# The whole decoder trunk put into one block that the scheduler orders on its detailed timing model

## The chip, the cores and the metric

The kernel runs on one core of a Trainium2 chip. The metric is the device time of one execution in microseconds (us). Three timed runs of the kernel before took 2652.8, 2655.67 and 2657.19 us; the median is 2655.67 us. Everything below that is called "the trace" comes from one further, profiled execution, whose first and last instruction are 2656.2 us apart.

## The reference, cut to what matters

The program is a decoder trunk of two layers over 1024 tokens of width 1024, all in float32. Each layer is a mixing sub-layer and a feed-forward sub-layer, and both take scale, shift and gate vectors from a condition vector `c`.

```
cond = silu(c)
for l in range(DEPTH):
    mod = cond @ w_mod[l] + b_mod[l]
    sh1, sc1, gt1, sh2, sc2, gt2 = split(mod, 6)
    h = rms_norm(x, norm_g[l, 0]) * (1.0 + sc1) + sh1
    y = mixer_block(h, ...)
    x = x + gt1 * rms_norm(y, norm_g[l, 1])
    h = rms_norm(x, norm_g[l, 2]) * (1.0 + sc2) + sh2
    y = square(relu(h @ w_up[l])) @ w_down[l]
    x = x + gt2 * rms_norm(y, norm_g[l, 3])
```

`mixer_block` projects `h` once and feeds four groups: a short gated convolution, an attention with a compressed, a selected and a window branch ("nsa"), a gated linear attention ("gla") and a gated MLP over 128 positions ("gmlp"). The four outputs are normalised, joined and sent through `w_o`.

## The kernel before, in words

**Tiling.** Tokens are cut into two halves of 512 (`hf` 0 and 1), and activations are held transposed, 128 features by 512 tokens. A matrix product is `gemm`: for each half of the weight rows `wunit` loads a 128x512 block (256 KB) by a DMA on SP's queue (L152), ScalarE rounds it to a high part (L161, CAST) and VectorE takes the low part by a subtraction (`sub`, L125). `mm3` (L167 to L169) then issues three matmuls of 512 columns for each block of 128 rows: high by high, high by low, low by high. So each weight unit of 12 matmuls needs one load, one ScalarE and one VectorE instruction before it. For a layer's mixer, `raw_a` or `raw_b` has 3 buffers and the split tiles 4; for the feed-forward `raw_f` has 4 and `w_f` 6.

**Stages.** The last lines of `trunk_kernel` (L961 to L975) give the program order: the mixer of layer 0 for half 0, then for half 1, a run of modulation columns, then feed-forward and mixer in turn: ff(0,0), mix(1,0), ff(0,1), mix(1,1), ff(1,0), ff(1,1). `mix` ends with the product by `w_o`, a root-mean-square norm (the matmul by `ones`, L189), `residual` (L134, L131) and the norm that makes the feed-forward's input. `ff` has 32 hidden groups: `up` makes one, `down` adds four of them to the eight output tiles `y`; it ends with the same norm and `residual`.

**Modulation columns.** `mod_col` computes 128 entries of `mod` on VectorE: two loads of 256 KB from `w_mod`, each followed by a multiply-and-reduce (L232, shown in the trace as CUSTOM_DVE_ANT_0 and in the order as ISA, with a second short instruction that reads the accumulator), and one small instruction (L134) that adds both and the bias. The first 32 reduces (`mw`, 12 buffers) come before anything else. The other 160 (`mr`, 2 buffers) are `mods(0, (2, 3, 4))` inside the first mixer, and `mods(0, (5,))` and `mods(1, range(6))` after the second: their results are needed only at the first residual and later.

**What sets the order.** The code is written stage by stage, and the Tile scheduler orders it. It walks a model of the machine through time and, on each engine, sends the ready instruction that stands earliest in program order (`high_priority` shifts this for some). The result is a fixed order for each engine's queue: on the chip an instruction waits until all before it on its engine have gone. SP's queue issues all loads and stores in one such order; a load that needs a free buffer holds up all the loads behind it.

Attention's last step is `attend`: four transposes of the weights through TensorE (L699), the cast of the result on ScalarE (L701), the low part on VectorE (L125), and two matmuls with the values (L704 for the high part, L705 for the low part).

Of the kernel before, what the change touches and what calls it, by code (L numbers as in the profile page):

```python
# [35 lines left out]
def trunk_kernel(ctx, tc, xT, c, pos, freq, sel, w_in, conv_w, cmp_pos, cmp_w1, cmp_w2,  # L36
                 gla_w2, gla_b, gmlp_ws, gmlp_b, gains, w_o, norm_g, w_mod, b_mod,
                 w_up, w_down, out):
    nc = tc.nc
    V, A, P, PE = nc.vector, nc.scalar, nc.gpsimd, nc.tensor  # L40
    dma = nc.sync.dma_start

# [12 lines left out]
    def ps(tag, shape=(128, 512)):  # L55
        return psum.tile(list(shape), F32, name="ps_" + tag, tag=tag,
                         bufs={"mm": 2, "ff": 2, "s": 2, "t": 1, "pv": 1}[tag])
# [9 lines left out]

    A.preload_act_table_set("natural_log_exp_and_others")

# [1 line left out]
    ident = const.tile([128, 128], F32, name="ident")  # L71
    ones = const.tile([128, 128], F32, name="ones")
    bones = const.tile([128, 128], F32, name="bones")
# [19 lines left out]
    P.affine_select(out=cm[:, 384:512], in_=cm[:, 384:512], pattern=[[-1, 128]],  # L93
                    compare_op=ALU.is_ge, fill=NEG, base=0, channel_multiplier=1)

# [1 line left out]
    par = []  # L97
    for l in range(DEPTH):
        d = {}
# [8 lines left out]
        for n in names:  # L108
            dma(out=par[l][n], in_=src[n][l])

# [1 line left out]
    KS = const.tile([128, 1024], F32R, name="KS")  # L112
    KW = const.tile([128, 1024], F32R, name="KW")
    VS = const.tile([128, 8, 128], F32R, name="VS")
# [5 lines left out]
    st_carry = const.tile([128, 64], F32, name="st_carry")  # L120
    V.memset(KC, 0.0)

# [1 line left out]
    def sub(out, a, b):  # L124
        V.tensor_tensor(out=out, in0=a, in1=b, op=ALU.subtract)  # L125

# [97 lines left out]
            add(yk, yk, xo(k)[:, cs])  # L224
            dma(out=xnew[:, k, cs], in_=yk)

# [1 line left out]
    def mod_col(l, j, k, mk):  # L228
        mp = work.tile([128, 2], F32, name="mp", tag="mp", bufs=4)
        for kh in range(2):  # L230
            raw = mk(w_mod[l, 8 * j + k, :, kh * T:kh * T + T], [128, T])
            V.tensor_tensor_reduce(out=raw, in0=raw, in1=cond[kh], scale=1.0, scalar=0.0,  # L232
                                   op0=ALU.mult, op1=ALU.add, accum_out=mp[:, kh:kh + 1])
        stt(par[l]["mod"][:, j, k:k + 1], mp[:, 0:1], mp[:, 1:2], par[l]["bmod"][:, 8 * j + k:8 * j + k + 1],
            ALU.add, ALU.add)
# [43 lines left out]
                mod_col(l, j, k, mk)  # L279
            mod_scale(l, j, slice(0, 8))  # L280

# [1 line left out]
    cosd = dram.tile([2, 128, T], F32, name="cosd")  # L283
    sind = dram.tile([2, 128, T], F32, name="sind")

# [43 lines left out]
                    A.copy(o, p)  # L329
                    dma(out=dst[hf], in_=o)  # L330

# [1 line left out]
    CONV0, GMLP0, GLA0, NSA0 = 0, 6, 10, 17  # L333

    def conv_part(l, hf, h, rg, lane, st_):
# [232 lines left out]
    def nsa_part(l, hf, h, rg, gates):  # L568
# [24 lines left out]
        A.copy(kvt[:, 16:528], p)  # L593
        if hf == 0:
            V.tensor_copy(cmp_halo, kvt[:, 512:528])
        # rotary embedding
        cos, sin = (rg.tile([128, T], F32, name="cs", tag="q", bufs=4) for _ in range(2))
        dma(out=cos, in_=cosd[hf])
        dma(out=sin, in_=sind[hf])
# [77 lines left out]
        for j in range(4):  # L677
# [53 lines left out]
            def gate(bi):  # L731
                return gates[:, j, :].rearrange("p (h b) -> p h b", b=3)[:, :, bi:bi + 1]

            # selected (every causal block) and window branches
            def branch(bi, KX, VX, pieces, far, h0, nh, last):
                two = far or len(pieces) == 2
                NM, L = small((128, nh, 2)), small((128, nh, 2))
# [53 lines left out]
            else:  # L791
                branch(1, KS, VS, [(0, 4), (4, i - 3)], False, 0, 4, False)
            branch(2, KW, VW, [(max(0, i - 3), min(i + 1, 4))], i >= 4, 0, 4, False)
            # compressed branch
            sp = ps("s", (128, 4, 64))
            for k in range(2):
                PE.matmul(sp[:, 2 * k:2 * k + 2, 0:ns], qs[:, k, tj], KC[:, :, 0:ns],
# [19 lines left out]
                add(yr, pr[64:128], yr)  # L817
        return [yN[:, 0, :], yN[:, 1, :]]

# [1 line left out]
    xa = [dram.tile([2, 128, 8, T], F32, name=f"xa{l}") for l in range(DEPTH)]  # L821
    xb = dram.tile([2, 128, 8, T], F32, name="xb")
    h2 = {}
# [10 lines left out]
    def mix(l, hf, h, between=None):  # L834
        d = par[l]
        gain = d["gain"]
        with ExitStack() as es:
            gr = es.enter_context(region("gates"))
            if l == 0 and hf == 0:
                sx = ("ff", "ff", "ff")  # L840
                with region("wb", "right") as lane_pool["b"]:
                    with region("gl", "right") as rg:
                        gates, lrT = gate_part(l, hf, h, gr, rg, "a")
                        rope_tables()
                        yn = nsa_part(l, hf, h, es.enter_context(region("ns")), gates)
                        ol = gla_part(l, hf, h, rg, "b", sx, lrT)
                    with region("cv", "right") as rg, region("gm", "right") as rg2:
                        og = gmlp_part(l, hf, h, rg2, "b", sx)
                        oc = conv_part(l, hf, h, rg, "b", sx)
                    mods(0, (2, 3, 4))  # L850
                lane_pool["f"] = pool("ff", side="right")
            else:
                sx = ("s", "t", "pv")
                with region("cv") as rg, region("gm") as rg2:
                    oc = conv_part(l, hf, h, rg, "a", sx)
                    og = gmlp_part(l, hf, h, rg2, "a", sx)
                with region("gl") as rg:
                    gates, lrT = gate_part(l, hf, h, gr, rg, "a")
                    ol = gla_part(l, hf, h, rg, "a", sx, lrT)
                yn = nsa_part(l, hf, h, es.enter_context(region("ns")), gates)  # L860
            on = group_out(yn, "t", gain[:, 2:4])
            outs = [split(t) for t in oc + og + ol + on]
# [200 lines left out]
```

## Time and profile before

| | |
|---|---|
| median of three timed runs | 2655.67 us |
| profiled execution, first to last instruction | 2656.2 us |
| TensorE matmul busy | 2513.5 us (95%), 11690 records |
| TensorE weight load busy | 1989.3 us (75%) |
| VectorE busy | 1680.0 us (63%) |
| ScalarE busy | 1310.3 us (49%) |
| GpSimd busy | 56.5 us (2%) |
| mean granted TensorE clock | 0.985 |
| DMA, mean over the span | 114 GB/s |

The page gives no other time of the profiled execution than its span, which is 0.5 us above the median. PE is TensorE's matmul, PEld its weight load, which runs beside it; DVE is VectorE, ACT ScalarE, POOL GpSimd, SP the engine that issues the DMAs. A busy time counts a stretch in which at least one instruction of the engine is in flight. The columns of each view are told at its first group below.

### The profile page before, as it was taken

Reading aid. Unit: us, or ns where it says so; the run is one execution under the profiler, and the core shown is the slowest. Engines: PE = TensorE matmul, PEld = TensorE weight load, DVE = VectorE, ACT = ScalarE, POOL = GpSimd, SP = SyncE. Lnnn points to the kernel's source line nnn. Section 1 sums busy time; section 2 is a strip of 40 time slices with the busy share of each in tenths; the row PEclk is TensorE's granted clock in tenths of the full one; section 3 lists DMA queues with packets and bytes.
Section 4 is the critical chain, followed back from the end, with each engine's and each line's share of the span. In section 5 each row is a group of like instructions: output and inputs, shape, how many; then the busy total and the mean of one; then the engine's idle time right before and its main releaser. Section 6 shows DMA issues by size and latency. Waiting matters only on the chain.

```text
span 2656.2 us, 34273 instructions
## 1 busy us (share of the span) xinstructions
PE 2513.5 (95%) x11690; PEld 1989.3 (75%) x11690; DVE 1680.0 (63%) x3540; ACT 1310.3 (49%) x2649; POOL 56.5 (2%) x65
## 2 busy tenths in 40 slices
PE   2899879999999999999999999999999999999998
PEld 1676657677778887767788887777777888788887
DVE  7797987888574448457674446547876544534446
ACT  3474534468654345356653435345775443434343
POOL 0100000200000000010000000001000000000000
PEclk9999989999999999999999999999999999999999
DMA  7435566511343334222243334222123333533332
GB/s 270 138 97 174 192 204 202 179 53 36 100 142 98 96 99 143 82 71 69 95 144 100 96 97 145 88 61 89 40 76 121 98 96 99 179 97 98 96 99 84
DMA packets 168937, 301.56 MB, mean 114 GB/s; under 512 B 20453, under 2 KB 24122, under 8 KB 168762
## 3 DMA queue, kind: packets, MB, share of 16 engines
q1 hardware_dynamic: 168762, 299.37, 36.3%
q8 instruction: 92, 1.51, 0.2%
q14 instruction: 83, 0.68, 0.1%
HBM read 281.47 MB, written 17.83 MB: 113 GB/s over the span
## 4 chain that ended last, share of the span: by engine, by line
PE 76%; DVE 10%; ACT 4%; DMA 4%; issue 2%; POOL 0%; DVEq 0%; SPq 0%; ACTq 0%; POOLq 0%
PE ps_ff L168 16%; PE ps_ff L169 16%; PE ps_ff L167 16%; PE ps_mm L167 6%; PE ps_mm L169 6%; PE ps_mm L168 6%; DMA mr<-in_w_mod_dram 3%; PE ps_pv L705 1%; PE ps_pv L704 1%; DVE mr L232 1%; PE ps_mm L699 1%; ACT bp L754 1%; PE ps_t L189 1%; PE ps_s L744 1%; DVE w_a L125 1%
## 5 line engine op out<-in xcount | busy, mean ns | idle before, releaser
L161 ACT CAST w_f<-raw_f 128x512 fp32r<-128x512 f32 x504 | 313.3, 622 | 649.7 <-PE ps_ff L168 638.6
L125 DVE TENSOR_TENSOR w_f<-raw_f,w_f 128x512 fp32r<-128x512 f32 x504 | 348.7, 692 | 261.6 <-ACT w_f L161 254.7
L169 PE MATMUL ps_ff<-h,w_f 128*128 128x512 f32 x1024 | 405.9, 397 | 17.1 <-DVE w_f L125 17.1
L167 PE MATMUL ps_ff<-h,w_f 128*128 128x512 f32 x1024 | 404.8, 396 | 4.8 <-ACT h L203 4.8
L168 PE MATMUL ps_ff<-h,w_f 128*128 128x512 f32 x1024 | 406.6, 397 | 0.6 <-DVE h L134 0.4
L167 PE MATMUL ps_ff<-hid,w_f 128*128 128x512 f32 x992 | 388.9, 392 | 0.1
L168 PE MATMUL ps_ff<-hid,w_f 128*128 128x512 f32 x992 | 388.6, 392 | 0.0
L169 PE MATMUL ps_ff<-hid,w_f 128*128 128x512 f32 x992 | 388.2, 391 | 0.0
L167 PE MATMUL ps_mm<-h,w_a 128*128 128x512 f32 x832 | 336.4, 405 | 34.8 <-ACT w_a L161 30.5
L169 PE MATMUL ps_mm<-h,w_a 128*128 128x512 f32 x832 | 332.7, 400 | 11.7 <-DVE w_a L125 11.6
L168 PE MATMUL ps_mm<-h,w_a 128*128 128x512 f32 x832 | 338.8, 409 | 0.9 <-DVE h L125 0.9
L131 DVE TENSOR_TENSOR y<-y,ps_ff 128x512 f32<-128x512 f32 (+1 forms) x232 | 154.9, 668 | 238.0 <-PE ps_ff L169 237.1
L161 ACT CAST w_a<-raw_a 128x512 fp32r<-128x512 f32 x208 | 128.6, 618 | 233.0 <-PE ps_mm L168 216.2
L169 PEld LDWEIGHTS ps_ff<-h,w_f 128*128 128x128 f32 x1024 | 195.0, 190 | 60.1 <-DVE w_f L125 18.8
L125 DVE TENSOR_TENSOR w_a<-raw_a,w_a 128x512 fp32r<-128x512 f32 x208 | 143.3, 689 | 152.2 <-ACT w_a L161 146.0
L167 PEld LDWEIGHTS ps_ff<-h,w_f 128*128 128x128 f32 x1024 | 195.4, 191 | 47.6 <-ACT h L203 6.5
L168 PEld LDWEIGHTS ps_ff<-h,w_f 128*128 128x128 f32 x1024 | 195.0, 190 | 45.2 <-issue 2.7
L167 PEld LDWEIGHTS ps_mm<-h,w_a 128*128 128x128 f32 x832 | 158.0, 190 | 81.2 <-ACT w_a L161 33.6
L167 PEld LDWEIGHTS ps_ff<-hid,w_f 128*128 128x128 f32 x992 | 186.6, 188 | 40.5 <-issue 1.4
L168 PEld LDWEIGHTS ps_ff<-hid,w_f 128*128 128x128 f32 x992 | 186.7, 188 | 39.1 <-issue 1.0
L169 PEld LDWEIGHTS ps_ff<-hid,w_f 128*128 128x128 f32 x992 | 186.7, 188 | 37.8 <-issue 0.5
L169 PEld LDWEIGHTS ps_mm<-h,w_a 128*128 128x128 f32 x832 | 157.9, 190 | 55.8 <-DVE w_a L125 15.1
(350 smaller groups left out, 3586.4 us busy)
## 6 DMA issues: line engine op xcount, KB each, us to landing
raw_f<-in_w_up_dram SPq DMA_DIRECT2D x256, 256.0 KB, 2.7
raw_f<-in_w_down_dram SPq DMA_DIRECT2D x256, 256.0 KB, 2.6
mr<-in_w_mod_dram SPq DMA_DIRECT2D x160, 256.0 KB, 3.0
raw_a<-in_w_in_dram SPq DMA_DIRECT2D x144, 256.0 KB, 2.8
raw_a<-in_w_o_dram SPq DMA_DIRECT2D x64, 256.0 KB, 2.9
mw<-in_w_mod_dram SPq DMA_DIRECT2D x32, 256.0 KB, 4.4
bp<-in_cmp_w_dram SPq DMA_DIRECT2D x32, 256.0 KB, 4.6
raw_b<-in_w_in_dram SPq DMA_DIRECT2D x32, 256.0 KB, 3.0
```

Source lines behind the costliest of these rows:

```text
L125: V.tensor_tensor(out=out, in0=a, in1=b, op=ALU.subtract)
L131: eng.tensor_tensor(out=out, in0=a, in1=b, op=ALU.add)
L161: A.copy(hi, raw)
L167: PE.matmul(ps_ap, wh, xh, start=start, stop=False)
L168: PE.matmul(ps_ap, wh, xl, start=False, stop=False)
L169: PE.matmul(ps_ap, wl, xh, start=False, stop=stop)
L189: PE.matmul(p, ones, acc, start=True, stop=True)
L232: V.tensor_tensor_reduce(out=raw, in0=raw, in1=cond[kh], scale=1.0, scalar=0.0, op0=ALU.mult, op1=ALU.add, accum_out=mp[:, kh:kh + 1])
L699: PE.transpose(tp[0:kn, hh, :], cols(h0 + hh), ident)
L704: PE.matmul(pv[:, h0:h0 + nh, :], vst, th[0:kn], start=first[0], stop=False)
L705: PE.matmul(pv[:, h0:h0 + nh, :], vst, tl[0:kn], start=False, stop=last)
L744: PE.matmul(sp[:, 0:w], qh[:, h0 + hh, :], KX[:, 128 * k0:128 * k0 + w], start=True, stop=False)
```

## The change

One line is added at the start of `trunk_kernel`. It opens a block that is closed when the function ends, and asks the scheduler to order what is traced in it on the timeline model instead of the plain one. No instruction is added or taken away, no tile changes its size or its number of buffers. The other eight hunks of the diff empty a comment line each, so the line numbers of the changed kernel are higher by one.

```diff
@@ -37,6 +37,7 @@
                  gla_w2, gla_b, gmlp_ws, gmlp_b, gains, w_o, norm_g, w_mod, b_mod,
                  w_up, w_down, out):
     nc = tc.nc
+    ctx.enter_context(tc.block(schedule_with_timeline_sim=True))
     V, A, P, PE = nc.vector, nc.scalar, nc.gpsimd, nc.tensor
     dma = nc.sync.dma_start
 
@@ -67,7 +68,7 @@
 
     A.preload_act_table_set("natural_log_exp_and_others")
 
-    # ---- constants ----
+
     ident = const.tile([128, 128], F32, name="ident")
...
```

All 11,105 matmuls of the program are the same and every engine's queue holds the same work in another order. Three places show how.

**VectorE, after the gates of the first mixer.** These rows follow VectorE's subtraction for `gates` (the last line of `logsig`). In the kernel before, weight splits (`w_a`, `w_b`) and attention's keys stand there; `mr` is a modulation reduce, `cond` its other factor, `mp` its sum.

```order
L134 SCALAR_TENSOR_TENSOR gates<-ps_t,gtmp 128x48
L125 TENSOR_TENSOR w_a<-raw_a,w_a 128x512 x2
L125 TENSOR_TENSOR w_b<-raw_b,w_b 128x512 x2
L590 MEMSET kvt 128x16
L595 COPY cmp_halo<-kvt 128x16
L125 TENSOR_TENSOR w_a<-raw_a,w_a 128x512 x2
L603 STREAM_SHUFFLE p<-p 128x512
L131 TENSOR_TENSOR p<-p 128x512
L613 CAST KS<-p 64x512
L615 CAST KW<-p 64x512
L125 TENSOR_TENSOR KS<-p,KS 64x512
L125 TENSOR_TENSOR KW<-p,KW 64x512
```

In the changed kernel the same place reads:

```order
L135 SCALAR_TENSOR_TENSOR gates<-ps_t,gtmp 128x48
L318 TENSOR_SCALAR sc<-n 128x8x8
L233 ISA mr,mp<-mr,cond_126 128x512
L233 ISA mp 128x1
L126 TENSOR_TENSOR w_a<-raw_a,w_a 128x512
L233 ISA mr,mp<-mr,cond_127 128x512
L233 ISA mp 128x1
L135 SCALAR_TENSOR_TENSOR mod_101<-mp,bmod_97 128x1
L126 TENSOR_TENSOR w_a<-raw_a,w_a 128x512
L233 ISA mr,mp<-mr,cond_126 128x512
L233 ISA mp 128x1
L126 TENSOR_TENSOR g<-g 128x512
```

Modulation reduces have moved up between the weight splits, and behind these rows nine more follow with only three small instructions between them. In both orders the first matmul of the first feed-forward stands as number 1164 on TensorE; ahead of it VectorE has 86 of the 160 `mr` reduces before and all 160 now. The rest of VectorE's work ahead of that matmul is the same, but for the small instructions that belong to those reduces.

**VectorE, at the end of the first feed-forward.** `y` with `G` is the scaling of `residual`, `y` with `xo` its addition, and each `w_f` is a weight split for the next feed-forward's matmuls, which TensorE has at this point. Before:

```order
L125 TENSOR_TENSOR w_f<-raw_f,w_f 128x512
L134 SCALAR_TENSOR_TENSOR y<-y,G_104,nt 128x512 x2
L131 TENSOR_TENSOR y<-y,xo 128x512 x2
L134 SCALAR_TENSOR_TENSOR y<-y,G_104,nt 128x512 x2
L131 TENSOR_TENSOR y<-y,xo 128x512 x2
L134 SCALAR_TENSOR_TENSOR y<-y,G_104,nt 128x512 x2
L131 TENSOR_TENSOR y<-y,xo 128x512 x2
L134 SCALAR_TENSOR_TENSOR y<-y,G_104,nt 128x512 x2
L131 TENSOR_TENSOR y<-y,xo 128x512 x2
L131 TENSOR_TENSOR nt<-nt 128x512
L125 TENSOR_TENSOR hid<-r,hid 128x512
```

And in the changed kernel:

```order
L126 TENSOR_TENSOR w_f<-raw_f,w_f 128x512 x2
L135 SCALAR_TENSOR_TENSOR y<-y,G_105,nt 128x512 x8
L126 TENSOR_TENSOR w_f<-raw_f,w_f 128x512
L132 TENSOR_TENSOR y<-y,xo 128x512 x4
L126 TENSOR_TENSOR w_f<-raw_f,w_f 128x512
L132 TENSOR_TENSOR y<-y,xo 128x512 x4
L126 TENSOR_TENSOR w_f<-raw_f,w_f 128x512
```

Before, sixteen residual instructions stood in one piece; now weight splits stand after the eighth, the twelfth and the sixteenth. The end of the second feed-forward reads the same in each order; at the end of the third the sixteen stand in one piece in both.

**TensorE, in the second mixer's attention.** `ps_t` and `ps_mm` with `ident` are transposes of attention weights, `ps_pv` the products with the values, `ps_s` the scores, and `ps_ff` the feed-forward of the other half. Before, in the second mixer:

```order
L704 MATMUL ps_pv<-w_a,VS 128x512
L699 MATMUL ps_mm<-ident,bp 128x128 x4
L765 MATMUL ps_s<-KW,qh 128x128
L766 MATMUL ps_s<-KW,ql 128x128
L705 MATMUL ps_pv<-w_a,VS 128x512
L704 MATMUL ps_pv<-w_a,VS 128x512
L699 MATMUL ps_t<-ident,bp 128x128 x4
```

In the changed kernel, in the third:

```order
L700 MATMUL ps_mm<-ident,bp 128x128 x2
L745 MATMUL ps_s<-KS,qh 128x384
L700 MATMUL ps_mm<-ident,bp 128x128 x6
L747 MATMUL ps_s<-KS,ql 128x384
L170 MATMUL ps_ff<-hid,w_f 128x512
L168 MATMUL ps_ff<-hid,w_f 128x512
L169 MATMUL ps_ff<-hid,w_f 128x512
L170 MATMUL ps_ff<-hid,w_f 128x512
L168 MATMUL ps_ff<-hid,w_f 128x512
L169 MATMUL ps_ff<-hid,w_f 128x512
```

Feed-forward matmuls now stand between the steps of attention, eight more of them behind the last row shown. In program order the feed-forward comes after the second mixer; before, a tenth of the first feed-forward's matmuls stood ahead of number 2133, now ahead of number 1619. The last 1635 matmuls, those of the last feed-forward, stand alone at the end in both.

## Rows read from the trace of the kernel before

**Rows 1.** The page, its head and part 1 (busy us, share of the span, instructions).

```profile
span 2656.2 us, 34273 instructions
...
PE 2513.5 (95%) x11690; PEld 1989.3 (75%) x11690; DVE 1680.0 (63%) x3540; ACT 1310.3 (49%) x2649; POOL 56.5 (2%) x65
```

**Rows 2.** Stretches (columns: length, each engine's busy us and instructions, TensorE clock, DMA).

```profile
0.00:361.30 361.30, 277.88 (x1313) 204.78 (x1313) 299.65 (x818) 182.33 (x397) 14.98 (x23) 0.96 0.56 179
361.30:560.00 198.70, 183.70 (x909) 136.98 (x909) 164.54 (x419) 86.43 (x180) 14.59 (x14) 0.97 0.55 172
560.00:2600.00 2040.00, 2007.69 (x9194) 1607.99 (x9192) 1180.03 (x2225) 1020.32 (x2031) 26.92 (x28) 0.99 0.32 97
...
850.00:900.00 50.00, 50.00 (x223) 41.40 (x222) 20.62 (x31) 20.05 (x34) 0.00 (x0) 1.00 0.33 97
```

**Rows 3.** Timeline of TensorE at the first feed-forward's first matmul (start us, duration, instruction).

```profile
361.28 1.22 PE L167 MATMUL ps_ff<-h,w_f 128*128 128x512 f32 x2 [3.52 <-ACT h L203]
```

**Rows 4.** Busy time of the mr tiles' instructions on VectorE, by stretch.

```profile
0.00:361.30 361.30, 59.29 (x86) 0.96 0.56 179
361.30:560.00 198.70, 51.31 (x74) 0.97 0.55 172
```

**Rows 5.** One tile, mr (durations min/median/max in ns, times; waits; landing).

```profile
L232 DVE CUSTOM_DVE_ANT_0 mr<-mr,cond x160: 647/686/1200, 82.2 to 544.5; 128x512 f32<-128x512 f32 x160
...
  DMA mr<-in_w_mod_dram: 36.6, 49
...
DMA to landing us min/median/max: 2.4/3.0/5.7
```

**Rows 6.** VectorE's waits to 361.3 us (total us, times, longest us).

```profile
DVE mr L232 <- DMA mr<-in_w_mod_dram: 18.7, 25, 2.0
DVE w_a L125 <- ACT w_a L161: 13.6, 4, 7.1
```

**Rows 7.** Waits of SP's DMA queue from 73 to 361.3 us.

```profile
SPq L275 <- DVE mp L232: 89.7, 61, 13.9
```

**Rows 8.** Timeline of VectorE around two reduces.

```profile
233.07 0.69 DVE L232 CUSTOM_DVE_ANT_0 mr<-mr,cond 128x512 f32<-128x512 f32 x1
...
233.68 0.68 DVE L392 TENSOR_REDUCE var<-sq 128x8 f32<-128x512 f32 x1
...
235.58 0.22 DVE L134 SCALAR_TENSOR_TENSOR mod<-mp,bmod 128x1 f32<-128x1 f32 x1
235.71 0.69 DVE L232 CUSTOM_DVE_ANT_0 mr<-mr,cond 128x512 f32<-128x512 f32 x1
```

**Rows 9.** Timeline of VectorE at the end of the first feed-forward.

```profile
1020.00 1.41 DVE L134 SCALAR_TENSOR_TENSOR y<-y,G,nt 128x512 f32<-128x512 f32 x2
...
1031.93 0.68 DVE L125 TENSOR_TENSOR w_f<-raw_f,w_f 128x512 fp32r<-128x512 f32 x1
```

**Rows 10.** Waits of TensorE over the span.

```profile
PE ps_ff L169 <- DVE w_f L125: 17.1, 4, 5.5
```

**Rows 11.** Timeline of TensorE at the same place as rows 9.

```profile
1026.79 0.39 PE L168 MATMUL ps_ff<-h,w_f 128*128 128x512 f32 x1
1032.66 0.80 PE L169 MATMUL ps_ff<-h,w_f 128*128 128x512 f32 x1 [5.49 <-DVE w_f L125]
1033.26 0.63 PE L167 MATMUL ps_ff<-h,w_f 128*128 128x512 f32 x1
1033.68 0.63 PE L168 MATMUL ps_ff<-h,w_f 128*128 128x512 f32 x1
```

**Rows 12.** Two stretches: that transition, and the third mixer's attention.

```profile
1010.00:1050.00 40.00, 34.52 (x136) 26.21 (x135) 33.37 (x53) 22.96 (x40) 0.00 (x0) 0.91 0.52 171
1050.00:1350.00 300.00, 294.19 (x1444) 228.33 (x1445) 184.14 (x422) 163.39 (x368) 12.55 (x13) 0.98 0.26 81
```

**Rows 13.** Timeline of TensorE in the second mixer's attention.

```profile
604.78 1.03 PE L699 MATMUL ps_mm<-ident,bp 128*128 128x128 f32 x8
...
606.12 0.48 PE L704 MATMUL ps_pv<-w_a,VW 128*128 128x512 f32 x1
```

## The prediction

> **What bounds the kernel now.** I began with the page's busy times. TensorE's matmul is busy for 2513.5 of 2656.2 us, its weight load for 1989.3 [rows 1]. The first figure suggests that no more than 143 us can be gained. To see whether a busy TensorE is also a fast one, I took a stretch inside the first feed-forward with nothing but its products: 223 matmuls in 50.00 us, one each 224 ns, with the weight load busy 41.40 us, 82.8% [rows 2]. I use that share as a yardstick: the weight-load time of a stretch, divided by 0.828, is an estimate of what its matmuls take undisturbed, and what the stretch takes beyond that I call excess.
>
> The Trainium skill ("Trainium Kernel Development and Optimization", section "Performance Expectations") calls matmul busy time a bad measure, since matmuls are pipelined, and weight-load time a good one. By the first, 32 us are to be had after 560 us, by the second 98; the trace agrees so far as the steady stretch shows 100% by the one and 82.8% by the other.
>
> The whole is 1989.3/0.828 = 2403 us of matmuls, so 253 us of excess. By stretch [rows 2]: up to 361.3 us, where the first feed-forward's first matmul starts [rows 3], 361.3 - 204.78/0.828 = 114 us; from there to 560 us, 198.7 - 136.98/0.828 = 33 us; to 2600 us, 2040 - 1607.99/0.828 = 98 us; the rest is the tail.
>
> What limits TensorE differs. Up to 361.3 us VectorE is busy 299.65 us, 83% [rows 2], and its largest wait is for the loads of `mr`, 18.7 us [rows 6]. From 361.3 to 560 us it is busy 83% again, and 51.3 of its 164.5 us belong to `mr` [rows 4]. After 560 us it is busy 58% and TensorE is the bound, with two kinds of loss: the ends of feed-forwards, and attention.
>
> **The early part.** The first feed-forward's first matmul is number 1164 on TensorE in both orders, so its time can be compared. VectorE does 86 `mr` reduces ahead of it before and 160 now. A further reduce with its accumulator read takes 0.61 us, from its start to the next instruction's [rows 8]: 74 x 0.61 = 45 us. Some 37 small sums of mod, one for two reduces, move up too, at 0.13 us [rows 8]: 5 us. The rest of VectorE's work ahead is the same: 300 + 50 = 350 us.
>
> To that come VectorE's waits. `mr` has two buffers: a load starts when the second reduce before it has ended, and lands after 2.4 to 5.7 us, median 3.0 [rows 5]. I went along each order of VectorE with the durations of the trace and let each reduce start no sooner than the landing after the end of the second reduce before it. With 3.0 us this gives 33 us of waits for the order before, in which the trace has 36.6 in 49 times [rows 5], and 43 us for the new one, where reduces stand in clusters, such as the fourteen with hardly anything between them shown in the change. Scaled by 36.6/33, that is 47; I take 45. With 2.4 us the walk gives 21 us, with 4.0 us, well inside the landings seen, 97. These are the bounds. A wait here also holds what is queued behind the reduce: weight splits, for which TensorE waits. And SP's queue is held by a load of `mr` without a free buffer, already 89.7 us in 61 times [rows 7], with the `raw` loads behind it.
>
> VectorE's other waits ahead of number 1164 are 361.3 - 299.65 - 18.7 = 43 us now, 13.6 of them for ScalarE's casts [rows 6]. With more work always ready in between some close: I take 25, between 10 (little more than the start of the program) and 43 (none closes). So number 1164 starts at 350 + 45 + 25 = 420 us, a loss of 59.
>
> **361.3 to 560 us.** This stretch loses 51 us of VectorE's reduces [rows 4], and the other 113 us are 57% of it. The steady stretch runs without excess at 20.62 of 50, 41% [rows 2]. So the excess of 33 us should mostly go; I leave 10 for attention and the clock: a gain of 23, bounds 15 and 33.
>
> **After 560 us.** At the first feed-forward's end VectorE does the sixteen residual instructions in one piece from 1020.00 us and reaches the next weight split at 1031.93 [rows 9]. TensorE stops for 5.49 us and then takes a matmul each 0.42 us, at a granted level of 1.2 GHz, for ten matmuls [rows 11]: 5.5 + 10 x 0.2 = 7.5 us. The three such places and one other wait make 17.1 us over the run [rows 10]. The stretch around the first has 40 - 26.21/0.828 = 8.3 us of excess [rows 12]. Two of the three ends now have splits between the residual's pieces, at most eight short instructions (8 x 0.61 = 5 us) apart, and the six tiles of `w_f` hold three units of 12 matmuls (36 x 0.224 = 8 us): nothing should stop there, a gain of 2 x 7.5, of which I take 14.
>
> The other 84 us lie mostly in the mixers that run beside a feed-forward: 300 - 228.33/0.828 = 24 us from 1050 to 1350 us [rows 12]. There the transposes of attention are followed by the matmul with the values after 1.3 us, three feed-forward matmuls beside them [rows 13], while the cast on ScalarE alone takes about 0.6 us. In the new order the median of TensorE's work between the last transpose and that matmul rises from 1.04 to 5.2 us (in matmuls at 224 ns; from the two orders). That covers the chain cast, low part, matmul, so I expect half of the 84 us, 41, back. Half, since the rest of the excess is short slow-clock stretches and matmuls of under 512 columns, which no order cures. Together 55 us. Bounds: 29 if only the visible idle time comes back (2040 - 2007.69 = 32 [rows 2], less 8 that stay, and 5 of the slow clock); 92 if all goes but the third end. The last 1635 matmuls stand as they did; the tail keeps its time.
>
> **Sum.** 59 - 23 - 55 = -19 from the profiled 2656.2, which lies 0.5 above the median: 2636 us. With the bounds of the late terms, and 45 held, the forecast's own range is 2612 to 2656.
>
> **Rivals.**
> 1. *The loads of `mr` land later.* Packed into the early part beside the weight loads (DMA share already 0.56 [rows 2]), all 160 land in 4.0 us rather than 3.0: 350 + 97 + 25 = 472 us, a loss of 111; 111 - 23 - 55 = +33: 2689 us. The change turns slower once the early loss passes 78 us, which is a landing of about 3.4 us. For it: landings up to 5.7 [rows 5], and the queue that is held for 89.7 us [rows 7]. Against it: the median of 3.0 was measured at that DMA share. The Trainium skill ("DMA: Bandwidth & Descriptors", section "Latency and other measured facts") says that the fixed part of a transfer grows from HBM's access time, 0.2 us on average and 2 us under high load. By that rule a denser stretch lands later; the trace's spread from 2.4 to 5.7 bears it out in kind, not in size.
> 2. *The early part is nearly free.* Loads land at the minimum, 21 us of waits, and the others shrink to 15: 350 + 21 + 15 = 386, a loss of 25; 25 - 23 - 55 = -53: 2603 us. For it: VectorE's other waits are chains that more work would fill. Against: fourteen reduces on two buffers can't hide their landing.
> 3. *The late excess isn't waits.* Only the visible idle comes back: 59 - 23 - 29 = +7: 2662 us. For it: TensorE's matmul is busy 98% after 560 us [rows 2]. Against: the excess sits in stretches with attention and is absent from 850 to 900 us.
>
> **How the numbers follow.** The forecast has 0.50, the first rival 0.20, the second 0.15, the third 0.15. A measurement of this kernel tells some 0.2%, 5 us, from no change. Of the forecast's half, 0.40 is faster by more, 0.08 the same and 0.02 slower; the first rival gives 0.17 slower and 0.03 the same; the second 0.15 faster; the third 0.08 same and 0.07 slower. Faster 0.55, same 0.19, slower 0.26. Both signs hold much, so the range goes from 2595 to 2690: it leaves out some 0.08 at each end.
>
> **What would show it.** Number 1164 should start near 420 us; under 390 is rival 2, over 440 rival 1. VectorE's waits for `mr` should total 45 us, all before that point, with a median landing near 3.0. In the 200 us after it the weight load's share should rise from 69% to near 79%. The wait of 5.5 us for `w_f` should stay once, at the end of the third feed-forward. From number 1164 on TensorE should need 78 us less than the 2295 it takes now. I am wrong if number 1164 comes later than 440 us, or if that later part gains under 55 us.

## The result and the profile after

The changed kernel takes 2682.7 us, median of four runs (2679.21 to 2686.41), the kernel before in the same session 2654.49. The ratio is 1.0107, 95% interval 1.0095 to 1.0119: slower by 28 us, where 19 us less had been forecast. The profiled execution is the fastest of the four (2679.21 us), so the traces show 21 of these 28 us.

The page of the changed kernel, its head and part 1, beside [rows 1]:

```profile
span 2677.5 us, 34062 instructions
...
PE 2515.8 (94%) x11690; PEld 2006.1 (75%) x11690; DVE 1674.8 (63%) x3540; ACT 1309.9 (49%) x2649; POOL 55.6 (2%) x65
```

Each engine has as many busy instructions as before; the 211 fewer in all are of the kinds that do not count as busy. The span is 21.3 us longer. Its stretches, cut at the same matmul as in [rows 2] (length, then busy us of PE, PEld, DVE, ACT, POOL, then clock, DMA share, GB/s):

```profile
0.00:419.90 419.90, 303.18 (x1313) 217.14 (x1313) 353.44 (x1008) 183.39 (x397) 15.26 (x23) 0.87 0.63 200
419.90:560.00 140.10, 140.10 (x663) 112.54 (x664) 67.75 (x107) 64.67 (x117) 0.68 (x1) 0.99 0.29 85
560.00:2620.00 2060.00, 2030.08 (x9452) 1638.01 (x9451) 1219.60 (x2349) 1042.25 (x2097) 39.64 (x41) 0.99 0.33 98
```

Number 1164, the first feed-forward's first matmul, starts here (timeline of TensorE, against [rows 3]):

```profile
419.87 1.22 PE L168 MATMUL ps_ff<-h,w_f 128*128 128x512 f32 x2 [2.98 <-ACT h L204]
```

So the early part loses 58.6 us. From there to the end the old kernel took 2656.2 - 361.3 = 2294.9 us, the new one 2677.5 - 419.9 = 2257.6: a gain of only 37.3. The reduces of `mr`, beside [rows 5]:

```profile
L233 DVE CUSTOM_DVE_ANT_0 mr<-mr,cond x160: 664/691/1302, 46.1 to 395.4; 128x512 f32<-128x512 f32 x160
...
  DMA mr<-in_w_mod_dram: 44.5, 55
...
DMA to landing us min/median/max: 2.5/3.0/6.0
```

They begin at 46 us instead of 82, VectorE waits 44.5 us for their loads, and a load lands as fast as before. What that does to TensorE is seen at its longest early stop for a weight split (timeline of TensorE, then of VectorE, around it):

```profile
86.05 0.39 PE L169 MATMUL ps_mm<-h,w_a 128*128 128x512 f32 x1
95.28 0.80 PE L170 MATMUL ps_mm<-h,w_a 128*128 128x512 f32 x1 [8.84 <-DVE w_a L126]
```

```profile
86.60 0.69 DVE L233 CUSTOM_DVE_ANT_0 mr<-mr,cond 128x512 f32<-128x512 f32 x1 [0.69 <-DMA mr<-in_w_mod_dram]
...
89.14 1.30 DVE L233 CUSTOM_DVE_ANT_0 mr<-mr,cond 128x512 f32<-128x512 f32 x1 [1.85 <-DMA mr<-in_w_mod_dram]
...
93.08 0.69 DVE L233 CUSTOM_DVE_ANT_0 mr<-mr,cond 128x512 f32<-128x512 f32 x1 [0.25 <-DMA mr<-in_w_mod_dram]
...
94.53 0.69 DVE L126 TENSOR_TENSOR w_a<-raw_a,w_a 128x512 fp32r<-128x512 f32 x1
```

The split that TensorE wants stands behind four reduces in VectorE's queue, three of which wait for their loads (the fourth, at 90.63 us, does not), and behind some work on attention's keys between them. TensorE has longer stops in the early part, the last of them 16.63 us at 414.8 us for the sums of a norm; the order without any reduces (e5 below) stops there for 13.77 us, so that one is mostly not theirs.

At the ends of the feed-forwards the wait for `w_f` of [rows 10] fell to 0.4 us, and another took its place (waits of TensorE):

```profile
PE ps_ff L168 <- ACT r L896: 22.4, 4, 12.6
...
PE ps_ff L170 <- DVE w_f L126: 0.4, 1, 0.4
```

The longest is at the end of the third feed-forward. TensorE there in the kernel before:

```profile
2301.12 0.79 PE L169 MATMUL ps_ff<-h,w_f 128*128 128x512 f32 x1 [4.28 <-DVE w_f L125]
```

TensorE, ScalarE and VectorE there in the changed kernel:

```profile
2310.31 0.39 PE L170 MATMUL ps_ff<-h,w_f 128*128 128x512 f32 x1
2323.25 0.80 PE L168 MATMUL ps_ff<-h,w_f 128*128 128x512 f32 x1 [12.55 <-ACT r L896]
```

```profile
2303.46 0.58 ACT L896 ACTIVATE r<-ps_ff 128x512 f32<-128x512 f32 x1
...
2317.78 0.62 ACT L899 CAST hid<-r 128x512 fp32r<-128x512 f32 x1 [6.13 <-DVE y L132]
2322.60 0.60 ACT L896 ACTIVATE r<-ps_ff 128x512 f32<-128x512 f32 x1 [4.20 <-DVE hid L126]
```

```profile
2311.77 5.38 DVE L135 SCALAR_TENSOR_TENSOR y<-y,G,nt 128x512 f32<-128x512 f32 x8
...
2317.07 4.89 DVE L132 TENSOR_TENSOR y<-y,xo 128x512 f32<-128x512 f32 x8
2321.89 0.68 DVE L126 TENSOR_TENSOR hid<-r,hid 128x512 fp32r<-128x512 f32 x1
```

Read it backwards. TensorE wants a result tile that ScalarE empties into `r`. There is one `r`, and it is free only when both halves of `hid` are made from it. The high half waits until 2317.78 us for a slot: the residual's loads `xo` use the same eight slots as `hid`, and only an addition frees one. The low half stands on VectorE behind all eight additions. So the relu that could have followed at about 2306 us (an estimate: the cast and the subtraction, 0.6 and 0.7 us, right behind ScalarE's square, which ends at 2305.07) comes at 2322.60.

To split the later part by kind, I summed the distances from each matmul's start to the next one's, from number 1164 on. It holds the same matmuls in each kernel; the last two columns are of e6 and e5 below, the two orders without reduces:

```
us, number 1164 to the last matmul    before  after   before   after
                                                      without  without
feed-forward, 512 columns (6048)      1442.8  1447.0  1431.7   1450.4
mixers' products, 512 columns (2112)   526.6   503.3   518.7    503.2
attention and the other small ones     276.3   255.0   278.1    253.5
last down product (192)                 26.2    29.5    26.2     29.9
norms by ones (49)                      12.6    11.1    12.6     11.1
sum                                   2284.5  2246.0  2267.3   2248.0
```

A stop of TensorE stands in this table with the matmul before it. Put with the matmul that waits, the step from the third column to the fourth is -51 us for the mixers (products and small ones) and +30 for the feed-forward, where the table has -40 and +19.

### The profile page after: what moved, and what is told of

It reads as the page before. It is cut to its first block, busy times and chain, and to the rows that moved or that the text cites. A ratio compares the mean times of both kernels' runs of the same rounds, so it can differ in the third digit from the quotient of the medians.

```text
span 2677.5 us, 34062 instructions
## 1 busy us (share of the span) xinstructions
PE 2515.8 (94%) x11690; PEld 2006.1 (75%) x11690; DVE 1674.8 (63%) x3540; ACT 1309.9 (49%) x2649; POOL 55.6 (2%) x65
## 4 chain that ended last, share of the span: by engine, by line
PE 80%; DVE 10%; DMA 6%; issue 2%; ACT 1%; SPq 0%; DVEq 0%; ACTq 0%
PE ps_ff L168 17%; PE ps_ff L169 17%; PE ps_ff L170 17%; PE ps_mm L168 6%; PE ps_mm L170 6%; PE ps_mm L169 6%; DMA mr<-in_w_mod_dram 5%; DVE mr L233 2%; PE ps_mm L700 1%; PE ps_pv L705 1%; PE ps_pv L706 1%; PE ps_s L745 1%; PE ps_s L747 1%; DVE y L132 1%; PE ps_t L190 1%
## 5 line engine op out<-in xcount | busy, mean ns | idle before, releaser
L168 PE MATMUL ps_ff<-h,w_f 128*128 128x512 f32 x1024 | 406.9, 398 | 25.5 <-ACT r L896 22.4
L168 PEld LDWEIGHTS ps_ff<-h,w_f 128*128 128x128 f32 x1024 | 194.4, 190 | 72.5 <-ACT r L896 24.6
```

Of the source, the lines that this page charges most:

```text
L168: PE.matmul(ps_ap, wh, xh, start=start, stop=False)
```

## Experiments

The first four ask which reduces cost, and what the ends cost.

**e1, e2: the late reduces behind the start of the feed-forward.** The core of the edit:

```diff
         for n in range(G):
             up(n)
+        if hook:
+            for t in cond:
+                stt(t, hid[G - 1][0].bitcast(F32), 0.0, t, ALU.mult, ALU.add)
+            hook()
...
-    mods(0, (5,))
-    mods(1, range(6))
-    xt = ff(0, 0)
+    xt = ff(0, 0, lambda: (mods(0, (5,)), mods(1, range(6))))
```

> The changed kernel, but the modulation columns that are first needed at the end of the first feed-forward (112 of the 160 mr reduces) are traced inside that feed-forward behind its fourth hidden group, and two small VectorE instructions tie them to it, so none can stand ahead of matmul 1164. Theory A (the early loss is VectorE's work and landing waits of the reduces moved up): 112 x 0.61 + 56 x 0.13 = 76 us of VectorE and about 31 us of its 44.5 us of waits leave the early part, less some 20 to 30 us of other waits that open again: matmul 1164 starts at 335 to 350 us instead of 420, and the whole takes 2595 to 2625 us. Rival B (the new order of the other early work, weight splits and loads, is the loss): matmul 1164 stays above 395 us and the whole above 2660.

Measured: 2677.59 us, number 1164 at 382.7. It gave back 37 us ahead of that matmul, and lost 33 behind it (sum of distances 2279.1 instead of 2246.0): most of it between 450 and 614 us, where the same reduces now stand in a clump beside the feed-forward; VectorE waits 71.0 us for the loads of all reduces, 51.1 of them behind 380 us. Neither theory's numbers came: 382.7 lies between A's 335 to 350 and B's 395, and the total is B's. What was moved costs about as much in its new place.

> The same shift in the kernel before, where 38 reduces less come ahead of matmul 1164. Theory A: 38 x 0.61 + 19 x 0.13 = 26 us of work and some 8 us of waits less, of which other waits take a part: matmul 1164 at 330 to 345 us instead of 361, the whole 2625 to 2645 us. So the changed order, with the reduces out of its way, is then the faster one by 15 to 35 us. Rival B: no gain here, and the changed kernel's shifted version not faster than this one.

Measured: 2704.91 us, ratio 1.0202 (1.0178 to 1.0226), number 1164 at 352.5. Theory A's numbers fail: 9 us are gained there and 55 lost behind, most of them from 712 to 820 us, where TensorE's longest stops are 8.78 and 17.25 us for a `w_f`. That e1 would be the faster of the two, by 27 us here, A had right. Of rival B the first half holds, the second does not. With the same 48 reduces ahead, the new order is 30 us later at number 1164 (382.7 against 352.5), so the first 48 cost as well in the place where it puts them.

**e3, e4: xo out of the hidden tiles' slots.**

```diff
-                     (lambda k: load(ffp.tile([128, T], F32, name="xo", tag="hid", bufs=8), xa[l][hf][:, k, :])),
+                     (lambda k: load(spare(), xa[l][hf][:, k, :])),
```

> The changed kernel with the residual's loads xo at the end of a feed-forward in tiles of their own (the h tag's, free by then) instead of in the eight slots of the hidden tiles hid. Theory C (the ends got slower because the next feed-forward's hidden tiles wait for slots that the residual's additions free, and these now stand behind all eight scalings): the waits of TensorE for the relu r (22.4 us, 4 times) fall under 12 us, the third end's 12.6 us under 6, the whole is 8 to 18 us shorter: 2665 to 2675. Rival D (VectorE's sixteen instructions in the way are enough by themselves): the waits stay within 4 us of 22.4 and the time within 5 us of 2683.

Measured: 2672.82 us, ratio to the kernel before 1.0073 (1.0058 to 1.0088), 10 us less than the changed kernel. Its profiled execution gains 10 us behind number 1164 (2235.9 instead of 2246.0) and loses 6 ahead of it, where nothing was edited (425.6 instead of 419.9). Behind it the feed-forwards' matmuls take 17.6 us less, and 7.3 come back at the norms. The wait for `r` is gone; this is the whole of it:

```profile
PE ps_ff L168 <- ACT r L896: 0.4, 1, 0.4
```

> The same edit in the kernel before, where TensorE waits at the three ends for weight splits w_f, 15.3 us, and not for r. Theory C: no change beyond 5 us (2649 to 2660), unless the scheduler now parts the sixteen residual instructions; then up to 20 us less. Rival D: the same time within 5 us.

Measured: 2655.0 us, ratio 1.0003 (0.9993 to 1.0012). Theory C holds for both: tiles of their own for `xo` are worth 10 us in the new order and nothing in the old one. The new tiles also let the scheduler order these places anew (at the third end the low halves of `hid` now stand ahead of the scalings), so e3 is more than the slots alone.

**e5, e6: none of the 160 reduces, and none of their loads.**

```diff
-            for k in range(8):
-                mod_col(l, j, k, mk)
+            V.memset(par[l]["mod"][:, j, :], 0.5)
```

> The changed kernel without any of the 160 mr reduces and their loads: the modulation columns that they make are filled with the constant 0.5. Theory A2 (all of the early loss is the reduces, the first 48 as well as the late 112, since both stand in clusters on two buffers): matmul 1164 starts at 315 to 340 us, as early as in the kernel before without them, and the whole is 25 to 45 us shorter than that one: 2570 to 2595 us. Rival B (the order of the other early work is slower by itself): matmul 1164 starts 20 us or more later than in the kernel before without reduces, and the two take the same time within 15 us.

> The kernel before without any of the 160 mr reduces, filled in the same way. Both theories: VectorE has 59 us of reduces and 19 us of waits for their loads less ahead of matmul 1164, part of which other waits take: it starts at 315 to 340 us instead of 361, and with the 51 us of reduces behind it gone too the whole is 2600 to 2630 us.

Measured: e5 2619.31 us, ratio 0.9866 (0.9851 to 0.9881); e6 2635.14, ratio 0.9929 (0.9914 to 0.9945). Number 1164 in e5 and in e6:

```profile
358.67 1.22 PE L168 MATMUL ps_ff<-h,w_f 128*128 128x512 f32 x2 [2.98 <-ACT h L204]
```

```profile
355.75 1.22 PE L167 MATMUL ps_ff<-h,w_f 128*128 128x512 f32 x2 [2.98 <-ACT h L203]
```

3 us apart, so rival B falls: the order of the other early work costs 3 us at most. Theory A2 is right that the two start alike, though both starts came 15 to 20 us later than I gave them, and too high on the whole: e5 is 16 us ahead of e6 and not 25 to 45. The reduces cost the old order 21 us and the new one 63, 61 of them ahead of number 1164; behind it the new order takes the same time with and without them (2246.0 and 2248.0).

**e7, e8, e12, e9: the reduces thinned out.** A pair of VectorE instructions of one column ties what follows to a result:

```diff
+    def tie(t):
+        for a in cond:
+            stt(a[:, 0:1], t, 0.0, a[:, 0:1], ALU.mult, ALU.add)
...
             hid[n] = (hi, lo)
+            for m in range(2):
+                if m == 0 and n < 28 and (l, hf) == (0, 0):
+                    tie(hi.bitcast(F32)[:, 0:1])
+                next(late, None)
```

`late` yields the 56 late columns one by one. In e9 the first 24 columns follow `tie(yn[0][:, 0:1])`, `tie(ol[0][:, 0:1])` and `tie(og[0][:, 0:1])`, eight each.

> The changed kernel with xo in the tiles of e3 and all reduces thinned out: the first 48 are tied behind the convolution of the first mixer, and the other 112 stand two columns (four reduces) behind each of the first 28 hidden groups of the first feed-forward, tied by two VectorE instructions of one column each. Theory A2: no clusters in the first mixer, matmul 1164 at 330 to 355 us, waits for the loads of mr beside the feed-forward hidden by its three units of split weights; the whole 2600 to 2630 us, faster than the kernel before by 25 us or more. Rival B: matmul 1164 stays at 375 us or later and the whole above 2645.

> The same thinning in the kernel before (xo as it was). Theory A2: matmul 1164 at 325 to 350 us, but there the feed-forward's split weights don't run ahead as well and the reduces beside it cost a part: 2625 to 2660 us. Rival B: the same or better than e7.

> As e7, but the first 48 reduces are left where the changed kernel has them (in clusters from 46 us on); only the late 112 are thinned out, and xo is in tiles of its own. It parts the two clusters. Theory A2: matmul 1164 near e1's 383 us, and none of the 33 us that e1 lost behind it: 2635 to 2645 us. Rival: the late reduces cost the same however they stand, 2660 to 2670 us (e1 less the 10 us of e3).

> As e7, but the first 48 reduces are tied in three parts: eight columns behind the attention, eight behind the gated linear attention and eight behind the gated MLP of the first mixer, so that they are done when its residual needs them. Theory A2 (clusters, and in e7 the first 48 standing too late, so that TensorE waited 26 us for the first residual's norm): matmul 1164 at 355 to 370 us instead of 385, the whole 2612 to 2630 us, faster than the kernel before by 1% or more. Rival B: matmul 1164 stays at 380 us or later, the whole at 2640 or more.

Measured: e7 2643.37 us, ratio 0.9959 (0.9945 to 0.9973), number 1164 at 384.9; e12 2637.87, 0.9933 (0.9915 to 0.9951), at 384.0; e9 2624.17, 0.9892 (0.9876 to 0.9908), at 371.1. e12 is what theory A2 gave; e7 meets neither expectation in full, since the first 48 came too late and TensorE waited 26.3 us for a norm. e9 came as expected, number 1164 one us late, and beats both kernels: 31 us under the one before, 58 under the changed one. Against e12 it differs in the place of the first 48 reduces alone, and its number 1164 is 13 us earlier. e8 took 2690.89 us and lost 1.35% (1.18 to 1.52%), worse than I gave it; as in e7 TensorE waits long for a norm (24.6 us), and number 1164 comes at 386.0.

**e10, e11: the reduces without their loads.**

```diff
-            t = work.tile(shape, F32, name="mr", tag="mr", bufs=2)
-            dma(out=t, in_=src)
-            return t
+            return work.tile(shape, F32, name="mr", tag="mr", bufs=2)
...
-            V.tensor_tensor_reduce(out=raw, in0=raw, in1=cond[kh], scale=1.0, scalar=0.0,
+            V.tensor_tensor_reduce(out=raw, in0=raw if own else cond[kh], in1=cond[kh], scale=1.0 if own else 0.001, scalar=0.0,
```

> The changed kernel with all 160 mr reduces but without their loads (each reduces cond by itself, scaled by 0.001). VectorE's work and place stay, the landing waits (44.5 us) and the block on SP's queue go. Theory E (the loss of 61 us is the landing waits on two buffers and what queues behind them): matmul 1164 comes down from 420 to 365 to 385 us, the whole to 2625 to 2650. Rival F (it is VectorE's work, 108 us, that TensorE waits for): matmul 1164 at 400 to 420 us, the whole 2660 to 2683.

> The same in the kernel before (all 160 reduces then stand ahead of matmul 1164 there too). Theory E: the reduces find free places on VectorE, matmul 1164 at 360 to 380 us, the whole 2635 to 2655. Rival F: matmul 1164 at 395 us or later, the whole above 2670.

Measured: e10 2671.05 us, ratio 1.0065 (1.005 to 1.008), number 1164 at 414.1: theory E fails, F holds here. e11 2656.65, ratio 1.0004 (0.9995 to 1.0014), at 365.0: F fails there, though VectorE has 155 of the reduces ahead of that matmul, and all 160 in e10. E has that start right for e11 and the whole 2 us too low. But the last five stand among the norm's rows right behind it, and TensorE stops once more (timeline of TensorE in e11):

```profile
364.97 0.50 PE L167 MATMUL ps_ff<-h,w_f 128*128 128x512 f32 x1 [2.98 <-ACT h L203]
...
377.88 0.79 PE L167 MATMUL ps_mm<-h,w_a 128*128 128x512 f32 x1 [10.81 <-ACT ah L340]
```

So in the old order the reduces cost 21 us in all without their loads (2656.65 - 2635.14), as much as with them. What differs between e10 and e11 is where they stand. From 60 to 240 us, where the first mixer's attention needs VectorE, its `mr` instructions in e10 and in e11 (length, busy us, count, clock, DMA share, GB/s):

```profile
60.00:240.00 180.00, 95.84 (x144) 0.81 0.18 57
```

```profile
60.00:240.00 180.00, 53.44 (x79) 0.96 0.21 66
```

Freed from the loads, the block's scheduler packed still more reduces into this stretch, so e10 did not take away a wait and leave all else. The runs side by side, by the time for which reduces hold VectorE there, busy or waiting for their loads:

```
60 to 240 us     mr busy  mr waits  longest  matmul records  number 1164
                    us       us       run     0 to 240 us     starts at us
e5  after, none     0        0         0         934           358.7
e6  before, none    0        0         0         922           355.8
e9  thinned        17.8      4.9       2         906           371.1
before             29.4      3.9       2         928           361.3
e2                 30.1      3.4       2         935           352.5
e12                28.9     18.4       7         791           384.0
e1                 29.6     19.6       7         795           382.7
e11 no loads       53.4      0         6         865           365.0
after              55.1     22.8       7         764           419.9
e10 no loads       95.8      0        34         684           414.1
```

The longest run is the number of reduces that start in this stretch with nothing of 0.3 us or more between them; the seven of the changed kernel hold VectorE from 71.3 to 84.5 us, the six of e11 from 216.3 to 221.4. e1 and e12 have as many reduces there as the kernel before and five times the waits, and they are 130 matmuls behind it at 240 us. Against the same order without reduces (e5 or e6), each microsecond held costs 2.2 to 3.0 matmul records in e1, e12, e10 and the changed kernel, 1.2 in e9, 1.1 in e11, and none in the kernel before and e2: the price goes with the place, and not with the amount or with the loads alone.

**e13, e14: which part of e9 counts.** e13 is e9 without the block, e14 is e9 with `xo` in the old slots.

> The edits of e9 (reduces thinned out and tied in three parts, xo in tiles of its own) in the kernel before, without the block. If the block's order of the rest is worth the 16 us that e5 and e6 showed, this takes 2630 to 2650 us. If thinning out is the whole gain of e9, 2620 to 2628. As e8 lost 36 us by thinning out, the plain order may place the tied reduces badly: then 2660 to 2690, and the thinning needs the block's order.

> e9 with xo back in the slots of the hidden tiles. If those slots are what made the ends of the feed-forwards slower, TensorE's waits for the relu r return (22.4 us, 4 times, the longest 12.6) and the time rises by 8 to 16 us: 2632 to 2640. If e3's gain was luck of the order, it stays within 5 us of 2624.

Measured: e13 2691.15 us, ratio 1.0127 (1.0109 to 1.0145): the same edits are 67 us better with the block's order. Of the 33 us by which its profiled execution is longer than that of the kernel before, 23 lie ahead of number 1164 (384.2 us) and 10 behind it, most of these between 792 and 827 us. Why the plain order places the tied reduces so badly I did not settle. e14 2643.14, ratio 0.9954 (0.9936 to 0.9973), 19 us over e9 and somewhat more than expected, and the wait is back:

```profile
PE ps_ff L168 <- ACT r L907: 24.4, 4, 12.6
```

In e9 that line reads:

```profile
PE ps_ff L168 <- ACT r L907: 1.1, 3, 0.5
```

## Why the prediction was wrong

**The early part: the sum right, its cause only half.** Forecast was number 1164 at 420 us with 45 us of waits for `mr` and a median landing of 3.0; measured 419.9, 44.5 and 3.0. VectorE's work came out at 353.4 for 350 and its other waits at 22 for 25, so that the hit to 0.1 us is in part two errors that cancel. Rivals 1 and 2 needed landings of 4.0 and 2.4, and fall. The Trainium skill ("DMA: Bandwidth & Descriptors", section "Latency and other measured facts") lets landing grow with the load on HBM; here the early stretch went from 179 GB/s [rows 2] to 200 and the median stayed at 3.0, so no run here shows it. But busy time and waits add up to the time of any stretch; the sum foretold the number, not what could be saved. e10 shows that taking the loads away does not bring 45 us back, and e11 that 155 reduces can stand ahead of that matmul at a cost of 9 us (365.0 against 355.8; 21 us in all with the five behind it). What costs, by the runs side by side and by e9 against e12, is VectorE held by reduces in clusters while the first mixer needs it; how the price divides between a cluster's length and its waits no run separates. I had counted what stands ahead of number 1164, and not where.

**361.3 to 560 us: near.** Forecast a gain of 23. The stretch behind number 1164 has next to no excess left: 140.1 - 112.54/0.828 = 4 us. The reduces behind number 1164 cost the old kernel 2284.5 - 2267.3 = 17 us, which are gone; in the new order that part is even 2 us longer without them (2248.0 for 2246.0). So they gave back 19 us for the 23. The weight load's share of the first 200 us is 158.06/200 = 79%, as forecast:

```profile
419.90:619.90 200.00, 200.00 (x972) 158.06 (x973) 97.80 (x180) 95.82 (x179) 4.82 (x8) 0.99 0.28 84
```

**Attention: right in kind.** Forecast 41 us. Between the orders without reduces the mixers' products lose 518.7 - 503.2 = 15.5 us and the small matmuls 278.1 - 253.5 = 24.6: 40, or 51 with each stop put to the matmul that waits. That half of the excess would come back stood on no row, so the near hit is partly luck. Rival 3, that only visible idle time comes back, falls: in front of these matmuls TensorE stood idle for 19.8 us in e6 and 2.4 in e5, so that 33 of the 51 came out of time in which it counted as busy. The Trainium skill ("Trainium Kernel Development and Optimization", section "Performance Expectations") calls matmul busy time a bad metric, because matmuls are pipelined, and weight-load busy share a good one; these runs agree.

**The ends of the feed-forwards: the step that failed.** I forecast a gain of 14, on the ground that splits now stand between the residual's pieces and that `w_f` has three units in store. That held for `w_f`: its wait fell from 17.1 us [rows 10] to 0.4. But I asked only what the removed wait was for, not what the next one would be. Putting eight scalings ahead of the additions holds the `xo` slots, these hold `hid`, `hid` holds the one `r`, and `r` holds TensorE: 22.4 us in place of 17.1, and at the third end 12.6 in place of 4.3. There I had one wait for `w_f` stay; it went too, and the wait for `r` came in its place. In the table without reduces the feed-forward's matmuls take 18.7 us more. Of these, 12 lie in gaps of over 0.26 us: 7 are the longer stops at the three ends (22.4 for 15.3), and most of the rest is two stops of 2.70 and 1.93 us near 1495 us of e5, whose cause stays open. The other 6.7 are a mean distance of 228.4 ns instead of 227.2, in matmuls that now run more beside the mixers; that this is why was not tested. e3 and e14 put the slots' part, with the reordering that they allow, at 10 and 19 us. The tail did not keep its time either: the last down product takes 3.7 us more.

The account closes: a gain of 14 forecast and 17 lost (18.7 - 1.5 at the norms) is 31 us, the tail 4, the reduces 4 (19 for 23) and attention 1: 40. Behind number 1164 a gain of 78 was forecast and 2284.5 - 2246.0 = 38.5 came; the miss in the span is 2677.5 - (2656.2 - 19) = 40. With each stop put to the matmul that waits, attention is 10 us better than forecast and the ends 11 worse than here. The chance was spread wrongly too: my slower rival was one of landings, and no rival had the ends go the other way. The forecast's own range does not follow from its bounds either: 59 - 33 - 92 = -66 and 59 - 15 - 29 = +15 give 2590 to 2671 us and not 2612 to 2656, and the result lies outside both.

## What to carry to other kernels

When a reordering takes a wait away, follow each tile that the moved instructions hold, through shared slots and single buffers, to the engine that waits for it: the next wait is often there. Time that off-path work takes from a helping engine has to be placed, not only added up: the same 48 reduces cost from nothing to 25 us at the first feed-forward, by where they stand. A scheduler that packs low-priority work into clusters can be kept from it by tying that work to results that come at the pace wanted; here that, with tiles of its own for `xo`, turned 1.1% of loss into 1.1% of gain. It has to be tried with each order: the same ties in the plain order cost 1.3%.

## What the runs showed of the hardware

In the changed kernel matmuls of 512 columns start 231 to 232 ns apart (median) from 900 to 950 us, where the mixers' products and a feed-forward's run mixed, and 227 ns apart from 2400 to 2450 us, where a feed-forward runs alone; TensorE is busy throughout at a granted clock of 1.00 in both. After the three stops at the ends of the feed-forwards, of 4.69, 4.69 and 12.55 us, the matmuls start 0.43 us apart for 3 to 5 us, as in [rows 11], at a granted clock of 0.50 to 0.52, the lower level of 1.2 GHz, before they are back at 0.23. The landing of a load of `mr` was steady: 2.4 or 2.5 us at least and 3.0 or 3.1 in the median in each of the twelve runs that have these loads, whatever the order.
